# First layer of a two-layer trunk: from the third input slab on, pairs of slabs as seven block products of scaled float16 pairs

## The chip, the core and the metric

One core of a Trainium2 chip runs the kernel. The metric is the device time of one execution in microseconds (us). The kernel before takes 1219.48 us (median of 3 runs, 1219.08 to 1220.45). TensorE is written PE (its weight loads PEld), VectorE DVE, ScalarE ACT, GpSimd POOL, and the engine that issues the DMAs SP.

## What is computed

Two layers over 1024 tokens of 1024 channels, in float32. The change touches the first layer alone:

```python
h = x @ w_in                      # 1024 x 1024 times 1024 x 3072
u_main, q_mem, g_main, g_mem = h[..., :1024], h[..., 1024:1536], h[..., 1536:2560], h[..., 2560:]
y_main = causal_multiscale_pool(u_main)        # 4 groups of 256 channels, windows 2, 4, 8, 16,
                                               # then a 256 x 256 map per group and a scale per channel
y_mem = memory_attention(q_mem, mem, w_mem_kv) # 4 heads into 256 memory tokens
y = concat([y_main * silu(g_main), y_mem * silu(g_mem)])
x = layer_norm(ALPHA * x + y @ w_out)
```

The second layer has the same projection, a forgetting attention of 16 heads in place of the pooling, and its own memory attention.

## The kernel before

Everything is kept transposed: channels lie on the 128 partitions and tokens along the free axis. `w_in` is cut into 24 slabs of 128 output channels for each layer: slabs 0 to 7 give `u_main` (two for each pooling group), 8 to 11 the memory queries, 12 to 19 the main gates, 20 to 23 the memory gates.

To keep float32 precision, each operand stands as a high part in a reduced float32 (`hi`, matmul type f32) and two bfloat16 tiles, the rest (`lo`) and a rounded copy (`top`). `hi_lo` (L160 on) makes them: two casts on ACT (L162, L164) and a subtraction on DVE (L163). A product is three: hi by hi, top by lo, lo by top (`three`). `slab` (L191 on) so issues 48 matmuls of 512 columns (L214): 2 halves of the tokens, 8 blocks of the inner dimension, 3 products. The weights of a slab come as two pieces of 128x512 through `split_w`: a DMA into the ring `raw` (4 tiles), then `hi_lo` into the ring `w` (6 tiles, two for a piece).

The first layer goes in this order. `load_x` brings the eight blocks of x, 512 KB each, and splits them, the `top` cast on POOL. `pool_group(0)` runs slabs 0 and 1 while x arrives, then the sums over the window (L554, a chain of additions of a tile with itself shifted, all on DVE), two gate slabs (12, 13) and the 256 x 256 map (L191, 24 matmuls). `mem_kv` projects keys and values of the memory tokens (eight projections of 24 matmuls of 256 columns, L248); `mem_attention` runs the four query slabs between them, and then the attention of eight token tiles, in which four gate slabs (20 to 23) fill PE between the steps of the softmax (`Fill.pump`). `pool_group(1)` to `(3)` follow, each with two slabs, two gates and its map; `OutProj.split` prepares pieces of `w_out` meanwhile (12 of 24 by the end of group 3, the rest in `OutProj.rest`), in tiles that `w_slots` takes from rings that are free by then (`wtags`, one of its entries, "PG", takes a tile of the rings P and G). `OutProj.rest` multiplies by `w_out` (L441), `norm` (L485 on, its tile `z` from the ring G, 4 tiles) normalizes and the result is transposed on PE (L294) as the input of the second layer.

Inside `mem_attention` the order on PE is the order of the program (`manual_schedule`); elsewhere, and on the other engines always, a scheduler orders the instructions before the run, by readiness in its own model and place in the program. On the chip every engine takes its instructions in that fixed order, and SP issues the DMAs in a fixed order too.

Of the kernel before, what the change touches and what calls it, by code (L numbers as in the profile page):

```python
# [9 lines left out]
F32 = mybir.dt.float32  # L10
# [8 lines left out]
P = 128  # L19
S = 1024  # L20
# [46 lines left out]
def run(units):  # L67
    for _ in units:
        pass
# [3 lines left out]
def trunk_kernel(ctx, tc, x, xT, memT, win, wk, wv0, wv, wmk, wmv, wout, poolw, pscale, lng, lnb, bforget, out):  # L73
# [24 lines left out]
    def sb(shape, tag, bufs, dt=F32, where=None):  # L98
        return (where or pool).tile(shape, dt, tag=tag, name=nm(tag), bufs=bufs)
# [4 lines left out]
    def G(shape=(P, S), dt=F32):  # L104
        return sb(list(shape), "G", 4, dt)

    def T(shape=(P, S), dt=F32R):
        return sb(list(shape), "T", 6, dt)

    def MK(shape, dt=F32R):  # L110
        return sb(list(shape), "MK", 4, dt)

    def raw(shape):
        return sb(list(shape), "raw", 4)

    def wt(shape, dt=F32R):
        return sb(list(shape), "w", 6, dt)
# [32 lines left out]
    def parts_of(make, shape):  # L150
        return Split(make(shape), make([shape[0], 2] + list(shape[1:]), BF16))
# [7 lines left out]
    def hi_lo(to, src, pinned=False, top=None):  # L159

        pin = tc.keep_in_program_order if pinned else lambda ins: ins
        pin(nc.scalar.copy(to.hi, src))  # L162
        pin(nc.vector.tensor_tensor(to.lo, src, to.hi.bitcast(F32), ALU.subtract))  # L163
        (top or nc.scalar.copy)(to.top, src)  # L164
# [6 lines left out]
    def split_w(src_dram, shape):  # L171
        r = raw(shape)
        nc.sync.dma_start(r, src_dram)
        to = parts_of(wt, shape)
        (gp_hi_lo if low[0] else hi_lo)(to, r)
        return to
# [43 lines left out]
                    yield NH  # L220

    SLAB = 48 * NH

    def gate(acc, dst):

# [80 lines left out]
    def gate_units(w_dram, dst, X):  # L306
        return slab(w_dram, X, lambda cols, acc: gate(acc, dst[:, cols]))

    def mem_attention(l, X, kv, qtile, ytile, yd):

        (mk, v, undo), keys, vals = kv
        qs = []
        if l:
            for h in range(MH):
                keys(h)
        for h in range(MH):
            while turns:
                spread()
            q = parts_of(qtile, [P, S])
            run(slab(win[l, 8 + h], X, lambda cols, acc: hi_lo(q[:, cols], acc)))  # L320
            qs.append(q)
            if not l:
                keys(h)
            vals(h)
        ys, gs = [ytile() for _ in range(MH)], [G() for _ in range(MH)]
        pt, fill = {}, Fill()
        for h in range(MH):
            fill.add(gate_units(win[l, 20 + h], gs[h], X), SLAB)

        def probs(i):  # L330

# [179 lines left out]

    X = parts_of(stream, [P, KT, S])

    def load_x(kt, parts=1):
        r = T(dt=F32)
        for i in range(parts):
            cols = slice(i * S // parts, (i + 1) * S // parts)
            nc.sync.dma_start(r[:, cols], xT[kt, :, cols])
            hi_lo(X[:, kt, cols], r[:, cols], top=gp_copy)

    first = [[split_w(win[0, 0, 0], [P, 4, P])], []]
    load_x(0, 2)
    first[1].append(split_w(win[0, 1, 0], [P, 4, P]))
    for kt in range(1, 4):
        load_x(kt)
    for f in range(2):
        first[f].append(split_w(win[0, f, 1], [P, 4, P]))
    for kt in range(4, KT):
        load_x(kt)
    nc.sync.dma_start(psc, pscale)  # L530
    nc.vector.tensor_scalar(pschalf, psc, 0.5, None, ALU.mult)
# [5 lines left out]
    with tc.tile_pool(name="in0", bufs=1) as in0:  # L537

        def bt(shape=(P, S), dt=F32R):
            return sb(list(shape), "B", 8, dt, in0)  # L540

        def pool_group(g):
            w = WINDOWS[g]
            pms = []
            for f in (2 * g, 2 * g + 1):
                u = sb([P, S], "P", 4)
                run(slab(
                    first[f] if g == 0 else win[0, f], X, lambda cols, acc: nc.scalar.copy(u[:, cols], acc),
                    ("L", 3) if f == 1 else ("pj", 2),
                ))  # L550
                cur, sh = u, 1
                while sh < w:
                    nxt = G()
                    nc.vector.tensor_tensor(nxt[:, sh:], cur[:, sh:], cur[:, : S - sh], ALU.add)  # L554
# [5 lines left out]
                nc.vector.tensor_tensor(pm[:, : w - 1], pm[:, : w - 1], u[:, : w - 1], ALU.subtract)  # L560
                pms.append(parts_of(T, [P, S]))
                hi_lo(pms[-1], pm)
            r = raw([P, 2, 2 * P])
            nc.sync.dma_start(r, poolw[g])
            w2 = parts_of(MK, [P, 2, 2 * P])
            hi_lo(w2, r)
            ys = []
            for f in (2 * g, 2 * g + 1):
                y = sb([P, S], "Y", 4, F32, in0)
                run(gate_units(win[0, 12 + f], y, X))  # L570
                ys.append(y)
# [22 lines left out]
        out_proj.rest(x, X1, x1)  # L594


    X = X1
    with tc.tile_pool(name="in1", bufs=1) as in1:
# [8 lines left out]
            return sb(shape, "V", 4, dt, in1)  # L607

        kv = mem_kv(1)
        mem_attention(1, X, kv, xy, lambda: vt([P, S], F32), y1d[2])  # L610
        cumd = dram.tile([HEADS, S], F32, name="cumd")
        fg = G((P, 8, ST * HEADS))
        flog = fg[:, 0, :]
# [406 lines left out]
```

## Time and profile before

| | |
|---|---|
| time, median of 3 runs | 1219.48 us |
| the profiled execution: its own time | 1218.15 us |
| its span, first to last instruction | 1216.4 us |
| PE busy | 1193.7 us (98%) |
| DVE, ACT, POOL busy | 793.3, 697.4, 221.0 us |
| POOL busy from 20 us to the end of the first layer | 0 |

The trace lists each instruction with its engine, line, start and length. A row of the view by lines gives a group's count, its busy time and the mean length of one in ns. Matmuls overlap in their pipeline, so the pace of a stream is read from the starts of successive rows and not from the length of one matmul. The stages of the first layer stand in the trace at: 0 to 32.5 us slabs 0 and 1 with the loading of x; to 59.1 the rest of group 0; to 123.3 queries and memory projections; to 187.5 the memory attention; to 330.5 groups 1 to 3; to 463 the output projection with the norm.

### The profile page before, as it was taken

What the parts mean: (1) busy time and instruction counts of PE and PEld (TensorE: products, weight loads), DVE (VectorE), ACT (ScalarE), POOL (GpSimd) and SP (SyncE); (2) the same over time, 40 slices, a digit from 0 to 9 for tenths busy, and PEclk for the clock granted to TensorE, in tenths of its full rate; (3) what the DMA queues carried; (4) which work ended last, traced back from release to release, by engine and by line L of the source; (5) the groups of instructions that cost most, each with busy time, mean ns of one, the idle gap of its engine ahead of it and who ended that gap; (6) DMA issues with size and microseconds to landing.
All of it is one profiled execution on the core that took longest, in us unless ns stands there. A gap on an engine that the chain in (4) does not pass through costs nothing. (4 is left out here: it accounts for less than half of the span.)

```text
span 1216.4 us, 20026 instructions
## 1 busy us (share of the span) xinstructions
PE 1193.7 (98%) x7018; PEld 758.7 (62%) x7018; DVE 793.3 (65%) x1853; ACT 697.4 (57%) x1474; POOL 221.0 (18%) x349
## 2 busy tenths in 40 slices
PE   9999999999999998999999999999999999999996
PEld 4566666555555666667686666666666666665553
DVE  7534676475644457357736888878877888874754
ACT  6556774374542345567533777767776777685220
POOL 4000000000000000000002454544444434640000
PEclk9999999999999999999999999999999999999999
DMA  6232553232452333234517879988887989895340
GB/s 229 84 112 95 122 131 139 95 121 88 164 182 104 111 129 116 70 96 109 159 52 181 162 161 194 181 187 172 182 195 159 193 188 229 222 241 195 132 156 36
DMA packets 267414, 178.68 MB, mean 147 GB/s; under 512 B 212272, under 2 KB 225712, under 8 KB 267312
## 3 DMA queue, kind: packets, MB, share of 16 engines
q1 hardware_dynamic: 267312, 177.40, 56.2%
q8 instruction: 55, 0.90, 0.3%
q14 instruction: 47, 0.39, 0.1%
HBM read 94.97 MB, written 22.61 MB: 97 GB/s over the span
## 5 line engine op out<-in xcount | busy, mean ns | idle before, releaser
L214 PE MATMUL pj<-A,w 128*128 128x512 bf16 (+1 forms) x2928 | 684.7, 390 | 3.1 <-DVE B L724 1.6
L214 PEld LDWEIGHTS <-w 128*128 128x128 bf16 x1984 | 182.3, 98 | 223.8 <-issue 23.3
L214 PEld LDWEIGHTS pj<-A,w 128*128 128x128 f32 x976 | 181.1, 189 | 45.8 <-ACT A L162 2.8
L789 ACT ACTIVATE T<-MK,s 128x512 f32<-128x512 f32 x192 | 111.3, 580 | 41.5 <-DVE s L781 23.6
L811 DVE SCALAR_TENSOR_TENSOR P<-T,s,P 128x512 f16<-128x512 f32 x192 | 111.6, 613 | 34.7 <-ACT P L810 33.4
L163 DVE TENSOR_TENSOR w<-raw,w 128x512 bf16<-128x512 f32 x106 | 75.6, 714 | 83.6 <-PE pj L214 51.5
L810 ACT ACTIVATE P<-T,s 128x512 f16<-128x512 f32 x192 | 103.0, 576 | 46.0 <-ACT T L789 20.1
L441 PEld LDWEIGHTS <-T 128*128 128x128 bf16 x736 | 70.7, 98 | 82.9 <-issue 3.7
L191 PE MATMUL L<-B,B 128*128 128x512 f32 (+3 forms) x384 | 105.8, 381 | 2.2 <-DVE s L781 2.1
L686 POOL MEMSET G<- 128x128 f32 x1 | 0.2, 208 | 581.5 <-ACT MK L164 581.5
L191 PEld LDWEIGHTS L<-B,B 128*128 128x128 f32 x384 | 70.8, 189 | 22.9 <-DVE s L781 4.8
L162 ACT CAST w<-raw 128x512 fp32r<-128x512 f32 x106 | 65.9, 621 | 26.6 <-PE pj L214 14.6
L157 POOL TENSOR_SCALAR w<-raw 128x512 fp32r<-128x512 f32 x108 | 67.3, 629 | 65.0 <-PE pj L214 59.7
L781 DVE CUSTOM_DVE_ANT_0 MK<-L,R 128x512 f32<-128x512 f32 (+3 forms) x128 | 72.5, 566 | 8.7 <-PE L L191 6.9
L164 ACT CAST w<-raw 128x512 bf16<-128x512 f32 x106 | 65.7, 620 | 18.9 <-PE pj L214 18.2
L773 POOL TENSOR_SCALAR_AFFINE_SELECT R<-R 128x128 f32<-128x128 f32 x128 | 41.3, 328 | 174.4 <-DVE s L781 129.4
L168 POOL TENSOR_TENSOR w<-raw,w 128x512 bf16<-128x512 f32 x54 | 69.6, 1288 | 18.7 <-PE pj L214 16.2
L163 DVE TENSOR_TENSOR T<-T,T 128x1024 bf16<-128x1024 f32 x23 | 28.0, 1218 | 52.2 <-ACT T L162 36.9
L833 PE MATMUL O<-T,V 128*64 128x128 f16 (+1 forms) x1152 | 57.6, 220 | 2.7 <-DMA T<-P 2.5
L833 PEld LDWEIGHTS <-V 128*64 128x64 f16 (+1 forms) x1152 | 50.2, 104 | 15.2 <-issue 5.7
L162 ACT CAST T<-T 128x1024 fp32r<-128x1024 f32 x23 | 24.1, 1046 | 60.3 <-DMA T<-y1d 33.9
L441 PE MATMUL pj<-B,T 128*128 128x512 bf16 (+1 forms) x192 | 52.6, 383 | 0.0
(230 smaller groups left out, 1699.3 us busy)
## 6 DMA issues: line engine op xcount, KB each, us to landing
raw<-in_win_dram SPq DMA_DIRECT2D x96, 256.0 KB, 2.8
raw<-in_wout_dram SPq DMA_DIRECT2D x40, 256.0 KB, 2.8
B<-B SPq DMA_DIRECT2D x32, 256.0 KB, 4.2
R<-cumd SPq DMA_DIRECT2D x16, 512.0 KB, 5.0
y0d<-Y SPq DMA_DIRECT2D x12, 512.0 KB, 3.1
T<-y0d SPq DMA_DIRECT2D x12, 512.0 KB, 3.8
T<-y1d SPq DMA_DIRECT2D x11, 512.0 KB, 4.9
raw<-in_wmk_dram SPq DMA_DIRECT2D x16, 256.0 KB, 2.6
```

The costliest lines, as they stand in the source:

```text
L157: nc.gpsimd.tensor_scalar(to, src, 1.0, 1.0, ALU.mult, ALU.mult)
L162: pin(nc.scalar.copy(to.hi, src))
L163: pin(nc.vector.tensor_tensor(to.lo, src, to.hi.bitcast(F32), ALU.subtract))
L168: nc.gpsimd.tensor_tensor(to.lo, src, to.hi.bitcast(F32), ALU.subtract)
L191: nc.tensor.matmul(acc, a, b, start=i == 0, stop=i == len(terms) - 1)
L214: nc.tensor.matmul(accs[n], a[:, k, :], b[:, pc * 4 + k, n * NH : (n + 1) * NH], start=seen[n] == 1, stop=seen[n] == 3 * KT,)
L441: nc.tensor.matmul(accs[a][nh], y, w, start=kt == 8 and i == 0, stop=kt == 7 and i == 2,)
L781: nc.vector.tensor_tensor_reduce(p[:, lo:up], lg, R[:, lo:up], 1.0, top, ALU.add, ALU.min, m[:, n : n + 1])
L789: nc.scalar.activation(e, p[:, lo:up], AF.Exp, bias=top, scale=-1.0, accum_out=sums[:, n, hd % 2, i : i + 1],)
L810: nc.scalar.activation(pair[:, lo:up], e, AF.Copy, scale=r)
L811: nc.vector.scalar_tensor_tensor(pair[:, L + lo : L + up], e, r, pair[:, lo:up], ALU.mult, ALU.subtract)
L833: nc.tensor.matmul(acc[rows, (i % 4) * P : (i % 4) * P + P], v[:, b, 2 * j : 2 * j + (1 if e else 2), :].rearrange("p e d -> p (e d)"), pt ...
```

## The change

Slabs 0 and 1 of the first layer stay as they were. The other 22 slabs go in eleven pairs. A pair is a product of 256 output channels by 1024 inner channels by 1024 tokens; it is cut into 2 x 2 blocks and done by seven block products in the place of eight (Strassen's scheme in Winograd's form). A block product is 128 outputs, 512 inner channels and 512 tokens.

The operands are now pairs of float16: a tensor is scaled by a power of two from its largest sum of absolute values, cast on ACT, and the rest taken by one DVE instruction (`halves_of`). Three products (high by high, high by rest, rest by high) make a block product 12 matmuls of 512 columns, and a pair 84.

- The blocks of x: seven combinations, made once (`combine`): 16 additions of 128x512 on POOL, and `halves_of` 28 times on 128x512. They lie in the tiles that held X. The blocks of x stay in the ring B till then.
- The blocks of the weights: for each pair four DMAs into `raw` (now 6 tiles), four ACT passes for the sums of absolute values, `bound` (a column of 128 maxima to DRAM and back to all partitions), four subtractions of 128x512 on POOL, and seven `halves_of` into `w` (now 8 tiles, one for a block).
- The results: running sums stay in PSUM where they can, and the others are read by ACT (2 for each pair) or by a DVE instruction that scales and adds (5 for each pair). The gate's tanh and product then work on SBUF tiles.
- The order: the eight memory projections now follow slabs 0 and 1 at once, each with a step of `combine`; the query pairs, gate pair and map of group 0 come behind them. In this stretch and in groups 1 to 3 PE's order is that of the program.
- Pooling: of the two window sums of a group the second runs on POOL (`pooled`).
- The output weights: 8 pieces by the end of group 3 in the place of 12; the ring W is gone, "PG" stands twice and the ring `w` twice in `wtags`.

```diff
+    def bound(sums):
+        m, e = tiny(1), tiny(1)
+        d = dram.tile([P, 1], F32, name=nm("bound"))
+        nc.vector.tensor_reduce(m, sums, AX.X, ALU.max)
+        nc.sync.dma_start(d, m)
+        every = sb([P, P], "every", 2, F32, more[0])
+        nc.sync.dma_start(every, d.rearrange("p o -> (p o)").partition_broadcast(P))
+        nc.vector.tensor_reduce(m, every, AX.X, ALU.max)
+        nc.vector.tensor_scalar(m, m, 2.0 ** -100, None, ALU.max)
+        nc.vector.tensor_scalar(e.bitcast(I32), m.bitcast(I32), 0x7F800000, None, ALU.bitwise_and)
+        return e
+
+    def scale_of(e, name):
+        sc = sb([P, 1], name, 3, F32, more[0])
+        nc.vector.reciprocal(sc, e)
+        nc.vector.tensor_scalar(sc, sc, 2.0 ** 12, None, ALU.mult)
+        return sc
+
+    def halves_of(to, src, sc):
+        nc.scalar.activation(to[:, 0], src, AF.Copy, scale=sc)
+        nc.vector.scalar_tensor_tensor(to[:, 1], src, sc, to[:, 0], ALU.mult, ALU.subtract)
+
+    def slab_pair(one, two, XC, dest, done):
+        combos, xun, ts = XC
+        b11, b12, b22, b21 = bs = [raw([P, 4, P]) for _ in range(4)]
+        sums = tiny(4)
+        for b, src in zip(bs, (one[0], two[0], two[1], one[1])):
+            nc.sync.dma_start(b, src)
+        for j, b in enumerate(bs):
...
+            nc.scalar.activation(junk, b, AF.Abs, accum_out=sums[:, j : j + 1])
+        e = bound(sums)
+        sc = scale_of(e, "wsc")
+        un = sb([P, 1], "wun", 3, F32, more[0])
+        nc.vector.tensor_tensor(un, e, xun, ALU.mult)
+        t1, t2, t3, t4 = ts
+        for to, a, b in ((t1, b12, b11), (t2, b22, t1), (t3, b22, b12), (t4, b21, t2)):
+            nc.gpsimd.tensor_tensor(to, a, b, ALU.subtract)
...
+        def plus(to, acc, other):
+            nc.vector.scalar_tensor_tensor(to, acc, un, other, ALU.mult, ALU.add)
...
+        steps = ((b11, "a", 1), (t2, "b", 1), (b21, "a", 0), (t1, "b", 0), (t3, "c", 1), (b22, "b", 0), (t4, "c", 0))
+        for k, (src, name, opens) in enumerate(steps):
+            w, xc = wt([P, 2, 4, P], F16), combos[k]
+            halves_of(w, src, sc)
+            if opens:
+                bank[name] = ps([P, NH], "pj", 2)
+            for i, (e0, e1) in enumerate(((0, 0), (0, 1), (1, 0))):
+                for kt in range(4):
+                    nc.tensor.matmul(
+                        bank[name], w[:, e0, kt, :], xc[:, e1, kt, :],
...
+                    if i == 2 and kt == 3:
+                        evac(k)
+                    yield NH
...
-                cur, sh = u, 1
+            for u, eng in zip(us, (nc.vector, nc.gpsimd)):
+                cur, sh = u, 1
                 while sh < w:
                     nxt = G()
-                    nc.vector.tensor_tensor(nxt[:, sh:], cur[:, sh:], cur[:, : S - sh], ALU.add)
-                    nc.vector.tensor_copy(nxt[:, :sh], cur[:, :sh])
+                    eng.tensor_tensor(nxt[:, sh:], cur[:, sh:], cur[:, : S - sh], ALU.add)
+                    eng.tensor_copy(nxt[:, :sh], cur[:, :sh])
...
+        for kt in range(KT):
+            junk = sb([P, S], "e", 3, BF16, in0)
+            nc.scalar.activation(junk, xs[kt], AF.Abs, accum_out=sums[:, kt : kt + 1])
+        e = bound(sums)
+        xsc = scale_of(e, "xsc")
...
+        quads = [sb([P, 4, 2, 4, NH], "A", 2, F16) for _ in range(2)]
...
+        changes = {0: ((b21, b21, b22, ALU.add), (b11, b21, b11, ALU.subtract)), 3: ((b21, b22, b11, ALU.subtract),), 2: ((b12, b12, b11, ALU.subtract),)}
+
+        def combine(k):
+            src = (b11, b11, b12, b21, b21, b12, b22)[k]
+            for kt in range(4):
+                halves_of(XC[0][k][:, :, kt, :], src[kt], xsc)
+            for to, a, b, op in changes.get(k, ()):
+                for kt in range(4):
+                    nc.gpsimd.tensor_tensor(to[kt], a[kt], b[kt], op)
+
+        with tc.manual_schedule(engines={PE}):
+            kv = mem_kv(0)
+            for h in range(2 * MH):
+                kv[1 + h // MH](h % MH)
+                if h:
+                    combine(h - 1)
+            pms = pooled(0, us)
+            qs = [parts_of(bt, [P, S]) for _ in range(MH)]
+            for h in (0, 2):
+                wide = [G() for _ in range(2)]
+                run(plain_pair(8 + h, wide, lambda j, cols, t: hi_lo(qs[h + j][:, cols], wide[j][:, cols])))
+            ys = [y_tile() for _ in range(2)]
+            run(gate_pair(12, ys))
+            pool_out(0, pms, ys)
+        mem_attention(qs, kv, lambda gs: [gate_pair(20 + h, gs[h : h + 2]) for h in (0, 2)], PAIR, y_tile, y0d[2])
 
-        wtags = [("B", 8)] * 4 + [("W", 4)] * 2 + [("MK", 4), ("w", 0)] + [("Y", 4)] * 2 + [("PG", 0), ("MK", 4)]
+        wtags = [("B", 8)] * 4 + [("MK", 4), ("w", 0), ("w", 0)] + [("Y", 4)] * 2 + [("PG", 0)] * 2 + [("MK", 4)]
         out_proj = OutProj(0, w_slots(wtags, in0), y0d)
-        pool_group(0)
-        kv = mem_kv(0)
-        mem_attention(0, X, kv, bt, lambda: sb([P, S], "Y", 4, F32, in0), y0d[2])
-        for g in range(1, 4):
-            pool_group(g)
-            out_proj.split((4, 12, 12)[g - 1])
+        with tc.manual_schedule(engines={PE}):
+            for g in range(1, 4):
+                us = [u_tile() for _ in range(2)]
+                run(plain_pair(2 * g, us))
+                pms = pooled(g, us)
+                ys = [y_tile() for _ in range(2)]
+                run(gate_pair(12 + 2 * g, ys))
+                pool_out(g, pms, ys)
+                out_proj.split((4, 8, 8)[g - 1])
```

More of the change, by code (lines that the diff above doesn't have):

```diff
@@ L321, in mem_attention @@
             qs.append(q)
-            if not l:
-                keys(h)
             vals(h)
+        return qs
+    def mem_attention(qs, kv, gates, cols_of_gate, ytile, yd):
+        mk, v, undo = kv[0]
         ys, gs = [ytile() for _ in range(MH)], [G() for _ in range(MH)]
         pt, fill = {}, Fill()
-        for h in range(MH):
-            fill.add(gate_units(win[l, 20 + h], gs[h], X), SLAB)
+        for units in gates(gs):
+            fill.add(units, cols_of_gate)
         def probs(i):
@@ new lines, in gate_pair, with done, plain_pair @@
+        def gate_pair(f, ys):
+            def done(j, cols, t):
+                y = ys[j][:, cols]
+                nc.scalar.activation(t, y, AF.Tanh, scale=0.5)
+                nc.vector.scalar_tensor_tensor(y, t, 1.0, y, ALU.add, ALU.mult)
+            return slab_pair(win[0, f], win[0, f + 1], XC, lambda j, cols: ys[j][:, cols], done)
+        def plain_pair(f, us, done=lambda j, cols, t: None):
+            return slab_pair(win[0, f], win[0, f + 1], XC, lambda j, cols: us[j][:, cols], done)
@@ new lines, in trunk_kernel @@
+        us = [u_tile() for _ in range(2)]
+        for f in range(2):
+            run(slab(
+                first[f], X, lambda cols, acc: nc.scalar.copy(us[f][:, cols], acc), ("L", 3) if f == 1 else ("pj", 2),
+            ))
+        sums = sb([P, KT], "xsums", 1, F32, in0)
+        for kt in range(KT):
[3 more added lines that the diff above has]
+        xsc = scale_of(e, "xsc")
```

125 lines of the change are left out of this document (85 added, 40 removed).

## The prediction

> **What bounds the kernel now.** I read the page's busy times first, then PE's timeline through the first layer, then the busy times by stage.
>
> ```profile
> span 1216.4 us, 20026 instructions
> PE 1193.7 (98%) x7018; PEld 758.7 (62%) x7018; DVE 793.3 (65%) x1853; ACT 697.4 (57%) x1474; POOL 221.0 (18%) x349
> ```
>
> ```profile
> 32.52 21.53 PE L214 MATMUL pj<-A,w 128*128 128x512 f32 x96
> 69.87 5.57 PE L248 MATMUL pj<-T,w 128*128 128x256 f32 x48
> 75.27 10.76 PE L214 MATMUL pj<-A,w 128*128 128x512 f32 x48
> ...
> 182.16 1.51 PE L191 MATMUL T<-T,MK 128*128 128x128 f16 x24
> 183.51 1.50 PE L191 MATMUL O<-T,MK 128*128 128x128 f16 x24
> 187.50 42.58 PE L214 MATMUL pj<-A,w 128*128 128x512 f32 x192
> 229.92 5.54 PE L191 MATMUL L<-T,MK 128*128 128x512 f32 x24
> 235.10 1.28 PE L214 MATMUL pj<-A,w 128*128 128x512 f32 x4
> ...
> 334.36 1.90 PE L441 MATMUL L<-B,T 128*128 128x512 bf16 x8
> 336.09 1.89 PE L441 MATMUL pj<-B,T 128*128 128x512 bf16 x8
> ```
>
> The columns are start, length, engine, line and count. Successive rows start where the last block's pace says they should: a group's 192 slab matmuls take 229.92 - 187.50 = 42.42 us, its map 5.18. PE waits for nobody here.
>
> ```profile
> 22.00:123.30 101.30, 100.47 (x550) 64.18 (x549) 48.26 (x91) 57.17 (x106) 0.00 (x0) 1.00 0.31 97
> 124.60:187.50 62.90, 62.90 (x471) 43.68 (x469) 45.54 (x112) 43.36 (x124) 0.00 (x0) 1.00 0.52 129
> 187.50:330.50 143.00, 143.00 (x652) 80.88 (x650) 85.83 (x131) 74.75 (x124) 0.00 (x0) 1.00 0.34 114
> ...
> 463.00:482.00 19.00, 15.05 (x113) 13.03 (x112) 15.21 (x33) 14.55 (x31) 0.00 (x0) 0.91 0.41 123
> ```
>
> Columns: stretch, its length, then the busy time of PE, PEld, DVE, ACT and POOL, the granted clock, DMA. PE fills the three stages that the change rewrites; DVE stands at 48, 72 and 60%, ACT at 56, 69 and 52%, POOL does nothing. What PE saves is saved outright, as long as DVE and ACT can carry what they are given.
>
> **What is saved on PE.** A pair of slabs now takes 42.42 / 2 = 21.2 us. Eight bfloat16 matmuls of 512 columns take 336.09 - 334.36 = 1.73 us, 0.216 each. For float16 the nearest row is the 24 matmuls of 128 columns in 183.51 - 182.16 = 1.35 us, 0.056 each, four of which make 0.225; I take 0.216 (the other end costs 0.8 us a pair). A pair then takes 84 x 0.216 = 18.15 us. Eleven pairs: 11 x 3.06 = **33.7 us** off PE, 9.2 in the first stage (three pairs), 6.1 in the memory attention, 18.4 in groups 1 to 3. PE alone would need 92, 57 and 125 us there.
>
> **What DVE gets.**
>
> ```profile
> L285 DVE SCALAR_TENSOR_TENSOR MK<-MK,s,MK 128x1024 f16<-128x1024 f32 x8 | 10.3, 1282 | 2.0 <-ACT MK L284 2.0
> L352 DVE SCALAR_TENSOR_TENSOR P<-P,s,P 128x256 f16<-128x256 f32 x32 | 13.4, 482 | 2.5 <-ACT P L351 2.5
> L163 DVE TENSOR_TENSOR w<-raw,w 128x512 bf16<-128x512 f32 x9 | 6.2, 690 | 2.5 <-PE pj L214 1.1 <-ACT w L162 1.0
> ...
> L163 DVE TENSOR_TENSOR w<-raw,w 128x512 bf16<-128x512 f32 x23 | 15.9, 691 | 21.5 <-PE pj L214 18.3 <-ACT w L162 3.2
> L554 DVE TENSOR_TENSOR G<-G 128x1022 f32<-128x1022 f32 x6 | 7.3, 1222 | 0.2
> L554 DVE TENSOR_TENSOR G<-P 128x1023 f32<-128x1023 f32 x6 | 7.3, 1218 | 0.0
> ...
> L554 DVE TENSOR_TENSOR G<-G 128x1020 f32<-128x1020 f32 x4 | 4.9, 1218 | 0.1
> ...
> L554 DVE TENSOR_TENSOR G<-G 128x1016 f32<-128x1016 f32 x2 | 2.4, 1214 | 0.0
> ...
> L802 DVE RECIPROCAL s<-s 128x1 f32<-128x1 f32 x128 | 20.8, 162 | 3.1
> ```
>
> The scaled subtraction of `halves_of` is the operation of L285 and L352: between 256 and 1024 columns it grows by 800 ns, so 512 take 0.75 us. `plus` is the same operation with PSUM as one source. A pair has 7 + 5 of them, 9.0 us, and seven short ones of the kind of L802, 1.1: 10.1 us. Back to back they overlap a little (L352: 32 x 0.482 = 15.4 us long, 13.4 busy), so I count 0.9 of that, **9.1 us a pair**, and for the 28 `halves_of` of x 28 x 0.75 x 0.9 = **18.9 us**. Gates keep their DVE instruction. What goes: the pieces of the weights (L163, 0.69 each: 12 in the first stage, the 9 and 23 of the rows in the others), half of the window sums (half of the rows' 21.9 us in groups 1 to 3, with nine short copies, 1.4 by L802's length; 1.4 in group 0) and four pieces of `w_out` (2.8). By stage:
>
> - first stage: 48.3 - 8.3 - 1.4 + 3 x 9.1 + 18.9 = 85 us
> - memory attention: 45.5 - 6.2 + 2 x 9.1 = 57.5 us, as long as PE's 57
> - groups 1 to 3: 85.8 - 15.9 - 11.0 - 1.4 - 2.8 + 6 x 9.1 = 109 us
>
> **What POOL gets, and what it does to DVE.**
>
> ```profile
> L168 POOL TENSOR_TENSOR w<-raw,w 128x512 bf16<-128x512 f32 x54 | 69.6, 1288 | 18.7 <-PE pj L214 16.2 <-POOL w L157 0.3
> ```
>
> An addition of 128x512 is 1.29 us on POOL (L168), one of 1024 columns at most two of them. First stage: 16 for x and 12 for three pairs, 36 us, with one window sum 38.7; memory attention 8, 10.3 us; groups 1 to 3: 24 and nine window sums, 54. Together **103 us**. By itself this hides everywhere. But see what happens when the two engines work at once, while x arrives:
>
> ```profile
> 7.84 1.05 POOL L157 TENSOR_SCALAR A<-T 128x1024 bf16<-128x1024 f32 x1 [1.32 <-DMA T<-in_xT_dram]
> ...
> 9.08 10.74 POOL L157 TENSOR_SCALAR A<-T 128x1024 bf16<-128x1024 f32 x6 [0.18 <-DMA T<-in_xT_dram]
> ...
> 13.98 1.52 DVE L163 TENSOR_TENSOR w<-raw,w 128x512 bf16<-128x512 f32 x1
> ...
> 17.39 1.52 DVE L163 TENSOR_TENSOR w<-raw,w 128x512 bf16<-128x512 f32 x1
> ...
> 22.02 1.21 DVE L163 TENSOR_TENSOR A<-T,A 128x1024 bf16<-128x1024 f32 x1
> ...
> 23.76 0.68 DVE L163 TENSOR_TENSOR w<-raw,w 128x512 bf16<-128x512 f32 x1
> ```
>
> A cast that takes POOL 1.05 us alone takes 10.74 / 6 = 1.79 beside DVE; a DVE subtraction that takes 0.68 alone takes 1.52. Each has waited for the other: they take turns. These subtractions read two tensors in SBUF, and so do `halves_of` (the source and the high part), the pooling, the memory pieces, L352 and the gates; `plus` reads one of its two from PSUM; I count it as free of this, and f rises if it isn't. The two-SBUF kind is about 160 of DVE's 252 us, an estimate from the lengths above: 105 `halves_of` 71, L352 13, 20 memory pieces 14, 24 gate products at 0.69 17, pooling, queries and output pieces 45. So some share f of POOL's 103 us adds to DVE's time. Bounds: 0, if POOL's instructions all fall into DVE's idle time and its PSUM work, and 1. If DVE were never idle, f would be near 160 / 252 = 0.64; it is idle at times; I take **0.5**.
>
> The Trainium skill, page "SBUF — State Buffer", section "SBUF: two separate sides", calls the port pair that the two engines share "an exclusive lock, not a bandwidth split", for a DVE instruction with two SBUF inputs against a GpSimd one that reads SBUF, held for the whole instruction. This trace agrees: 0.68 + 0.84 = 1.52.
>
> **The sum.** First stage: 85 + 0.5 x 38.7 = 104 us of DVE from 22 us on. The tiles of X can't be rewritten before the last matmul of slabs 0 and 1 at 32.5 us, which leaves DVE some 6 us idle. ACT is nearly as full.
>
> ```profile
> L162 ACT CAST w<-raw 128x512 fp32r<-128x512 f32 x106 | 65.9, 621 | 26.6 <-PE pj L214 14.6 <-DMA raw<-in_win_dram 5.7 <-DMA raw<-in_wmk_dram 2.3
> L789 ACT ACTIVATION_READ_ACCUMULATOR T<-MK,s 128x1 f32 x192 | 36.5, 190 | 0.2
> L162 ACT CAST T<-G 128x1024 fp32r<-128x1024 f32 x8 | 8.4, 1046 | 5.1 <-DVE G L560 5.1
> ```
>
> 57.2 in its row, less 24 casts (14.9), and 28 x 0.62 for x (17.4), 8 x (1.05 + 0.19) for its sums (9.9) and three times 4 x 0.81 + 7 x 0.62 + 2 x 0.6 (26.4): 96 us, and each high part precedes its rest on DVE. Two engines that wait on each other at 90% don't mesh; I add 8 us. The stage ends at 22 + 104 + 6 + 8 = 140 us, where it ended at 123.3: **+17** (26 lost against PE's 92). PE waits in the projections and the first query pair.
>
> Memory attention: 57.5 + 5 = 62.7 against 62.9: **0**. Groups 1 to 3: 109 + 27 = 136 against 143: **-7**. Output projection: four more pieces to prepare behind group 3, and "PG" twice leaves `norm` two z tiles of four where it had three, so that the fourth row block's x is fetched only once a z is transposed. The nearest rows are the wait that follows this stage, 19 us with PE busy for 15.05, and nothing at all; I take **+4**. Together +14 on the profiled execution's 1218.15, 1232. The median of the runs is 1.3 above that execution, so **1233 us**.
>
> That stage shows a clock of 0.91 where PE idled; the Trainium skill, page "TensorE: Matmul & The Clock Gate", Part 1, has the clock halve after an idle window of about 3.4 us. By it the waits of the first stage would cost somewhat more; nothing above counts it.
>
> **The rivals.**
>
> 1. *PE stays the bound.* POOL's additions have a pair's time to be done (`w` holds 8 tiles, a pair needs 7), so they may fall where DVE reads PSUM or idles. For it: 160 + 103 us of turn-taking just fit under PE's 274. Against it: DVE alone is level with PE in the memory attention. Price: f near 0.15, and in the first stage ACT's 96 us from 22 us on, 4 above PE's 92, with 6 for X: -33.7 + 10 + 4 = -20, **1199 us**. It decides from f = 0.36 down, since each tenth of f is 10 us.
> 2. *No meshing at all.* The order on DVE is fixed before the run; where a subtraction stands at its head while POOL holds the port, the PSUM reads behind it wait too, and PE waits for its bank. f near 1: +14 + 51 = **1284 us**; with f = 0.8, 1264.
> 3. *The scale of each pair comes late.* `bound` puts two DMAs in a row on SP's queue, and the DVE reduction behind them holds up DVE's queue.
>
> ```profile
> cumd<-G SPq DMA_DIRECT2D x8, 8.0 KB, 2.0
> bfb<-in_bforget_dram SPq DMA_DIRECT2D x1, 8.0 KB, 2.6
> ```
>
> Four sums 3.2, two DMAs 4.6, short work 1.1 and a first high part and rest 1.4: 10.3 us for each pair. I hold it hidden, since the rings hold a pair ahead of 18 us. With no cover: 11 x 10.3 = 113 less 33.7, about **1299 us**.
> 4. *float16 doesn't keep bfloat16's pace:* 11 x 0.8 us more on PE, little here, where PE is not the bound.
>
> **How the numbers follow.** The forecast has 0.48, the first rival 0.27, the second 0.17, the third 0.05, the fourth 0.03. A measurement tells about 0.2%, 2.4 us, from no change. The forecast's own range is f from 0.3 to 0.7, 1213 to 1253; most of it is slower (0.43), a little the same (0.03) or faster (0.02). With the first rival faster 0.30, same 0.04, slower 0.66. The range for 8 in 10 takes in most of the first rival and the lower half of the second: 1201 to 1265.
>
> **What would show it.** Right: DVE near 90% busy, its waits included, from 30 us to the end of group 3; `halves_of` beside POOL above 1.2 us where alone it takes 0.75; POOL's additions stretched past 1.29; PE gaps in the memory projections and the first query pair, released by ACT and DVE; the first matmul of L441 near 340 us. Wrong: seven block products in 18.2 us back to back in groups 1 to 3 (first rival), or PE waiting at each pair's first product for a DVE instruction that waits for a DMA (third).

## The result, and the profile after

The changed kernel takes **1399.97 us** (median of 4 runs, 1395.51 to 1403.29) against 1219.28 for the kernel before (4 runs): **1.148 times** as long, 95% interval 1.144 to 1.152. That is slower, as forecast, but by 181 us where 14 were predicted, and far outside the range. The profiled execution took 1397.46 us.

First the page of the changed kernel: span, busy times, and two of the rows of 40 slices (tenths).

```profile
span 1395.8 us, 20190 instructions
PE 1202.3 (86%) x6886; PEld 726.7 (52%) x6886; DVE 908.1 (65%) x2033; ACT 758.4 (54%) x1605; POOL 337.1 (24%) x429
...
PE   8635857557776689998999999999999999999997
...
PEclk9777988788998889999999999999999999999999
```

PE stands idle for 1395.8 - 1202.3 = 193.5 us, where it stood idle for 1216.4 - 1193.7 = 22.7: 171 us more. No other engine is full. And PE's busy time rose by 8.6 us where 33.7 were to be saved: the slices with holes in PE are also those with a clock of 0.7 to 0.9, most of them 0.7 and 0.8. The work itself keeps the pace that was predicted. The timeline of PE for one pair (start, length, engine, line, count):

```profile
139.14 5.34 PE L314 MATMUL pj<-A,wx 128*128 128x512 f16 x24
144.32 1.89 PE L314 MATMUL pj<-A,w 128*128 128x512 f16 x8
```

24 matmuls in 144.32 - 139.14 = 5.18 us, 0.216 each. So float16's pace is not why PE's busy time misses its saving by 42 us; the lower clock is what the page shows beside it. After a wait the same work is slower: at 427.91 us, behind a wait of 9.81, 24 such matmuls take 7.09 us, and the granted clock between 427.9 and 435.3 us is 0.71. The stages (busy time of PE, PEld, DVE, ACT and POOL, clock, DMA; the first row is the stretch from 22 us to the first matmul of the memory attention, then one window within it, then the attention, then groups 1 to 3):

```profile
22.00:191.90 169.90, 111.74 (x521) 59.37 (x519) 102.16 (x174) 89.81 (x169) 45.78 (x31) 0.81 0.31 58
50.00:100.00 50.00, 28.30 (x161) 20.83 (x159) 45.17 (x74) 39.08 (x73) 22.46 (x15) 0.74 0.26 79
191.90:299.40 107.50, 62.62 (x458) 38.94 (x456) 59.83 (x135) 52.41 (x146) 14.66 (x11) 0.79 0.39 69
299.40:501.80 202.40, 140.65 (x580) 60.78 (x578) 132.08 (x203) 90.35 (x161) 54.78 (x38) 0.85 0.35 80
```

The three stages grew by 69, 43 and 59 us (from 101.3, 64.2 and 143.0), what comes behind them by 8. In none is an engine near full over the whole stage: this is waiting, in a place with little slack. The view of the waits of 90 to 500 us says on what (engine, line, released by: us in total, times, longest; waits of POOL and PEld are left out):

```profile
...
DVE s L242 <- DMA every<-bound: 72.4, 10, 13.4
ACT wx L254 <- DVE wsc L250: 48.8, 4, 14.6
...
PE pj L314 <- ACT wx L254: 43.0, 2, 22.5
...
PE pj L314 <- ACT w L254: 36.2, 2, 22.7
...
PE pj L314 <- DVE e L279: 22.0, 7, 6.0
...
PE pj L314 <- DVE s L243: 9.8, 1, 9.8
```

Read it as a chain: PE waits for ACT's first high part (L254), ACT for the scale (L250), DVE for the load in `bound` (L242). PE also waits for DVE instructions that have nothing to do with the scale (L279, the reading of a bank). Not all of that is the exchange's: 16.5 of these 22.0 us lie in groups 1 to 3, where the kernel without the exchange (experiment 1) has 17.3 for the same instruction. But a DVE instruction that waits for the exchange holds up whatever stands behind it in DVE's fixed order: at 371.88 us L242 has waited 6.91 us for its load, and PE then goes on after a wait of 5.65 us for an instruction behind it (L680, which reads the bank of the map). The exchange itself, in the view of the tile `bound` (count, ns to issue, first and last; who waited; from issue to landing, store and load together):

```profile
L239 SPq DMA_DIRECT2D bound<-s x12: 319/329/562, 31.1 to 444.6; - x12
L241 SPq DMA_DIRECT2D every<-bound x12: 320/326/327, 38.6 to 452.4; - x12
...
  DVE s L242: 81.3, 11
...
DMA to landing us min/median/max: 3.3/6.0/9.4
```

The first store is issued at 31.1 us and its load at 38.6: 7.5 us in between; over the twelve the distance is 7.2 to 9.4, and from the store to the reduction 11.6 to 13.3. The prediction had 4.6 for both DMAs. What a single exchange does in groups 1 to 3 stands in the timeline:

```profile
320.67 0.33 SPq L239 DMA_DIRECT2D bound<-s  x1
321.10 1.06 SPq L508 DMA_DIRECT2D raw<-in_wout_dram  x2
...
322.39 5.34 PE L314 MATMUL pj<-A,w 128*128 128x512 f16 x24
...
328.60 0.33 SPq L241 DMA_DIRECT2D every<-bound  x1
331.52 0.62 ACT L171 CAST B<-raw 128x512 fp32r<-128x512 f32 x1 [8.25 <-DMA raw<-in_wout_dram]
...
332.18 0.69 DVE L172 TENSOR_TENSOR B<-raw,B 128x512 bf16<-128x512 f32 x1 [8.71 <-ACT B L171]
...
333.18 0.28 DVE L242 TENSOR_REDUCE s<-every 128x1 f32<-128x128 f32 x1 [0.31 <-DMA every<-bound]
...
334.19 0.74 DVE L279 SCALAR_TENSOR_TENSOR e<-pj,wun,e 128x512 f32<-128x512 f32 x1
...
334.98 2.29 PE L314 MATMUL pj<-A,w 128*128 128x512 f16 x5 [7.25 <-DVE s L244]
```

PE's block ends at 327.73. The read of its bank (L279) comes only at 334.19, and PE goes on when it is done, at 334.93 (the trace puts the wait down to L244, which ends at about the same moment). Two things stand before that read in DVE's order. The first is the subtraction for a piece of `w_out` (L172), for which DVE waits 8.71 us: the loads of `w_out`, issued at 321.10 behind the store, are late, and the ACT cast before the subtraction waits 8.25 us for one. The second is the reduction of the *next* pair's scale, for which DVE then waits only 0.31 us more. So here the store does its harm through the loads behind it; at 394.36 and 455.27 us ACT waits 6.36 and 11.23 us for such loads in the same way. The view of the DMAs of 320 to 334 us has their times from issue to landing:

```profile
raw<-in_wout_dram SPq DMA_DIRECT2D x3, 256.0 KB, 10.3
every<-bound SPq DMA_DIRECT2D x1, 64.0 KB, 4.5
bound<-s SPq DMA_DIRECT2D x1, 0.5 KB, 7.9
```

A store of half a kilobyte takes 7.9 us, and loads issued behind it 10.3, where the median over the run for such a load is 3.1.

### The profile page after: what moved, and what is told of

It is laid out like the page before. It is cut to its first block, busy times and chain, and to the rows that moved or that the text cites. A ratio compares the mean times of both kernels' runs of the same rounds, so it can differ in the third digit from the quotient of the medians.

```text
span 1395.8 us, 20190 instructions
## 1 busy us (share of the span) xinstructions
PE 1202.3 (86%) x6886; PEld 726.7 (52%) x6886; DVE 908.1 (65%) x2033; ACT 758.4 (54%) x1605; POOL 337.1 (24%) x429
## 5 line engine op out<-in xcount | busy, mean ns | idle before, releaser
L223 PE MATMUL pj<-A,w 128*128 128x512 bf16 (+1 forms) x1872 | 448.6, 391 | 5.3 <-ACT A L171 2.4
L314 PE MATMUL pj<-A,w 128*128 128x512 f16 x696 | 172.8, 410 | 87.8 <-ACT w L254 36.2
L223 PEld LDWEIGHTS <-w 128*128 128x128 bf16 x1264 | 114.0, 98 | 140.6 <-issue 19.4
L314 PEld LDWEIGHTS <-w 128*128 128x128 f16 x696 | 72.3, 104 | 184.6 <-issue 78.6
L978 DVE SCALAR_TENSOR_TENSOR P<-T,s,P 128x512 f16<-128x512 f32 x192 | 111.5, 613 | 34.8 <-ACT P L977 33.5
L223 PEld LDWEIGHTS pj<-A,w 128*128 128x128 f32 x624 | 115.2, 190 | 31.0 <-ACT A L171 4.6
L314 PE MATMUL pj<-A,wx 128*128 128x512 f16 x228 | 54.3, 394 | 46.4 <-ACT wx L254 43.0
L347 PE MATMUL pj<-T,w 128*128 128x256 bf16 (+1 forms) x336 | 51.5, 307 | 23.5 <-ACT w L173 6.9
L172 DVE TENSOR_TENSOR T<-T,T 128x1024 bf16<-128x1024 f32 x23 | 28.1, 1223 | 58.4 <-ACT T L171 36.4
L172 DVE TENSOR_TENSOR w<-raw,w 128x512 bf16<-128x512 f32 x55 | 42.0, 764 | 32.1 <-PE pj L223 14.8
L314 PEld LDWEIGHTS <-wx 128*128 128x128 f16 x228 | 22.8, 101 | 75.6 <-ACT wx L254 43.8
```

The lines of the kernel that those rows point to most:

```text
L223: nc.tensor.matmul(accs[n], a[:, k, :], b[:, pc * 4 + k, n * NH : (n + 1) * NH], start=seen[n] == 1, stop=seen[n] == 3 * KT,)
L314: nc.tensor.matmul(bank[name], w[:, e0, kt, :], xc[:, e1, kt, :], start=bool(opens) and i == kt == 0, stop=k in (2, 5, 6) and i == 2 and k ...
L978: nc.vector.scalar_tensor_tensor(pair[:, L + lo : L + up], e, r, pair[:, lo:up], ALU.mult, ALU.subtract)
```

## The experiments

The theory: the exchange of the scale sets the time, through its own length and through the queues that it holds. The rivals: the turns that POOL and DVE take (the prediction's own term), and plain work on ACT or DVE. Ratios are to the kernel before on the same chip, with the 95% interval; differences are given in us of 1219.

**1. No exchange.** `bound` keeps its first reduction and gives a constant.

```diff
-        nc.sync.dma_start(d, m)
...
-        nc.vector.tensor_scalar(e.bitcast(I32), m.bitcast(I32), 0x7F800000, None, ALU.bitwise_and)
+        nc.vector.tensor_scalar(e, m, 0.0, known, ALU.mult, ALU.add)
```

> The exchange of the maximum over the partitions through DRAM is left out: the sums and the first reduction stay, and the scale is a constant, the one that the exchange gives for this data (512 for x, 8 for each pair). In the changed kernel each of the 12 exchanges takes 11.6 to 13.3 us from the store's issue to the reduction of what came back, and DVE stands at that reduction. Theory A (the exchange, by the queues that it holds, is what PE waits for): 120 to 160 us fall away, 1240 to 1280. Theory B (DVE and GpSimd in turn, as the prediction has it): at most 40 us, 1360 or more. Theory C (the preparation of a pair starts too late whatever it holds): about half, 1310 to 1340.

1292.4 us, 1.061 [1.059, 1.064]: 106 us of the 181 are the exchange. The time lies between the ranges of theories A and C.

**2. The exchange made, its result unused.** Constant scale as in 1, but both DMAs and the reduction stay.

```diff
         nc.vector.tensor_reduce(m, sums, AX.X, ALU.max)
+        nc.vector.tensor_scalar(e, m, 0.0, known, ALU.mult, ALU.add)
         nc.sync.dma_start(d, m)
```

> The exchange stays in its queues, two DMAs on SP and the reduction on DVE, but nobody uses what it brings: the scale is the constant of the run without it. Theory A1 (the exchange hurts because the instruction that waits for it holds up DVE's and SP's queues): most of the loss stays, 1340 to 1390. Theory A2 (it hurts because the scale comes late): the time of the run without the exchange, within 15 us.

1355.1 us, 1.112 [1.110, 1.115]. So of the 106 us, 62 are there though nobody needs the scale (what waits behind the exchange on DVE, on SP and among the DMAs), and 44 come with the lateness of the scale itself.

**3. The additions of W back on DVE**, with the exchange (`e3`) and without (`e4`).

```diff
-            nc.gpsimd.tensor_tensor(to, a, b, ALU.subtract)
+            nc.vector.tensor_tensor(to, a, b, ALU.subtract)
```

> The 44 subtractions of W move from GpSimd to DVE, where one takes about 0.69 us; the exchange stays. Theory A: DVE waits idle for the exchange and has room, so 1385 to 1415, as the changed kernel within 1%. Theory B: the turns with GpSimd fall away in the pairs, 80 us or more, 1320 or less.

> Both edits: no exchange and the subtractions of W on DVE. Against the run without the exchange alone this prices the turns that DVE and GpSimd take in the pairs: by the prediction's f of 0.5, 57 us of GpSimd work cost 28 us and 30 us of DVE work come back, so the two are within 10 us of each other; if the port doesn't matter, this run is 10 to 25 us slower.

1393.3 us, 1.144 [1.141, 1.146], whose interval overlaps that of the change; and 1286.2 us, 1.056 [1.054, 1.058], 6 us below experiment 1. Having W's additions on GpSimd costs some 6 us, with the exchange and without.

**4. No sums at all.** No exchange, no ACT passes for the sums, a constant set by a memset.

```diff
-            nc.scalar.activation(junk, b, AF.Abs, accum_out=sums[:, j : j + 1])
...
-        nc.vector.tensor_reduce(m, sums, AX.X, ALU.max)
...
+        nc.vector.memset(e, known)
```

> Without the exchange, and the passes that sum absolute values are left out too (four on ScalarE for a pair, eight for x, and their reductions): the scales are constants that wait for nothing. Theory C1 (what is left, 73 us over the kernel before, is a pair's preparation that starts late, since the sums stand late in ScalarE's order): 40 us or more below 1292, 1250 or less. Theory C2 (it is the work on DVE and GpSimd in the first stage): ScalarE loses 45 us of work, DVE next to nothing, 10 to 20 us, 1270 to 1282.

1264.5 us, 1.037 [1.035, 1.039]: 29 us below experiment 1 and between the ranges of C1 and C2. The passes are 4 x 0.81 us for each pair on ACT, but the next experiment keeps them and wins nearly as much.

**5. The sums in a ring of their own**, on top of 1.

```diff
-        sums = tiny(4)
+        sums = sb([P, 4], "wsums", 3, F32, more[0])
```

> Without the exchange, and a pair's tile of four sums gets a ring of its own. In the kernel it comes from the ring of four tiles from which each softmax step takes all four (maximum, scaled maximum, sum, reciprocal), so that a gate pair that is emitted behind a softmax step can't start its sums before that step is over: in the run without the exchange they start at 162.8 us, as the last exponential ends, though the weights have long landed. Theory C1 with this cause: the waits of 9.6 and 8.0 us at the start of the two gate pairs of the memory attention go, 12 to 25 us, 1267 to 1280, and the stage (158.4 to 245.4 us there) shrinks to 62 to 75 us. Theory C2: nothing, 1288 to 1297.

1267.9 us, 1.040 [1.039, 1.042], 25.6 us below experiment 1 from this one line. `tiny(4)` shares a ring of four tiles with the softmax of the memory attention. The timeline of experiment 1 shows it:

```profile
162.72 0.21 ACT L440 ACTIVATION_READ_ACCUMULATOR P<-L,s 128x1 f32 x1
162.82 0.64 ACT L260 ACTIVATE A<-raw 128x512 bf16<-128x512 f32 x1
...
167.35 1.26 POOL L267 TENSOR_TENSOR A<-raw,raw 128x512 f32<-128x512 f32 x1 [37.00 <-ACT A L260]
```

The sums of the next gate pair (L260) begin as soon as the softmax's last exponential has been accumulated (L440), and POOL has been waiting for them for 37 us. With its own ring the memory attention takes 68.1 us instead of 84.9.

**6. Other work away from GpSimd**, each on top of 1: the second window sum (`e7`), the additions of x (`e8`), and all of it, with W's additions and the ring of 5 (`e9`).

```diff
-            for u, eng in zip(us, (nc.vector, nc.gpsimd)):
+            for u, eng in zip(us, (nc.vector, nc.vector)):
...
-                    nc.gpsimd.tensor_tensor(to[kt], a[kt], b[kt], op)
+                    nc.vector.tensor_tensor(to[kt], a[kt], b[kt], op)
```

> Without the exchange, and the second window sum of a group goes back from GpSimd to DVE: ten additions of 1024 columns, 1.22 us each on DVE, over 2 us on GpSimd. If the turns of the two engines set the time of groups 1 to 3, 5 to 15 us are won, 1277 to 1287; if DVE's own work does, 5 to 12 us are lost, 1297 to 1305.

> Without the exchange, and the 16 additions for x on DVE: 11 us of DVE work for 20 us of GpSimd work in the first stage. If the chain through GpSimd and the turns set the start of the first query pair (94.6 us in the run without the exchange), it comes 5 to 12 us earlier, 1280 to 1287; if DVE's own work does, it comes up to 10 us later, 1295 to 1303.

> Without the exchange, own ring for the sums, and all three kinds of work that the change gave to GpSimd on DVE (additions of W, additions for x, second window sums). Added up from the single runs: 1268 less 6, 6 and 15, so 1241. If the turns of the two engines overlap with other waits and the three shares aren't additive: 1247 to 1260. Below 1219 only if the first stage's wait goes too, which nothing here touches but the additions for x.

1277.2 us, 1.048 [1.046, 1.050]; 1286.6, 1.056 [1.054, 1.058]; and with all of it 1239.4, 1.017 [1.015, 1.019], 28.4 us below experiment 5; the single shares, 6 (`e4`), 16 and 7, add up to it. DVE gets more to do and the kernel is faster. The turns are one reason. Another is that the work itself gets shorter (a subtraction of W takes 1.26 us on POOL and 0.68 on DVE) and that POOL drops out of the chain; no run separates the two, though no wait of PE in the change or in experiment 5 is put down to POOL. `halves_of` in the views of its line, first the changed kernel, then `e9` with GpSimd idle in the whole stretch (ns, min/median/max):

```profile
L255 DVE SCALAR_TENSOR_TENSOR w<-A,wsc,w x35: 739/747/2384, 114.4 to 467.5; 128x512 f16<-128x512 f32 x35
L255 DVE SCALAR_TENSOR_TENSOR A<-B,xsc,A x28: 733/742/1833, 49.4 to 92.3; 128x512 f16<-128x512 f32 x28
```

```profile
L249 DVE SCALAR_TENSOR_TENSOR w<-A,wsc,w x35: 739/746/753, 88.0 to 317.4; 128x512 f16<-128x512 f32 x35
L249 DVE SCALAR_TENSOR_TENSOR A<-B,xsc,A x28: 736/744/753, 39.9 to 79.9; 128x512 f16<-128x512 f32 x28
```

Alone 0.75 us, never more; beside GpSimd up to 2.4.

**7. With the exchange: its own ring (`e12`), and GpSimd idle too (`e10`).**

> The changed kernel with one edit, the own ring for the sums, exchange and GpSimd work kept. If the ring costs what it costs without the exchange: 1370 to 1380. If the sums' late start in the memory attention exposes the whole exchange there (waits of 22.7 and 20.7 us): 1345 to 1365.

> As the run with no GpSimd work and the own ring, but with the real exchange through DRAM. If the exchange costs what it cost in the changed kernel (108 us): 1345 to 1355. If half of that cost came from the late start of the gate pairs of the memory attention, whose sums now start earlier: 1300 to 1330.

1359.6 us, 1.116 [1.114, 1.119], and 1335.6 us, 1.097 [1.094, 1.099]. The ring costs 39 us here, against 26 without the exchange, and `e12` lies in the second of its ranges: the late start of the sums exposes part of the exchange too. GpSimd's work costs 24 us, about what it cost without (28). Taking both away doesn't hide the exchange: `e10`, between its two ranges, and `e9` differ in the exchange alone and lie 98 us apart.

**8. What of the exchange is slow.** Its store writes one float of each of 128 partitions. As 128 rows of 512 bytes (`e11`, on top of 2, one run), and as 4 rows of 128 bytes, after a transposition on DVE, with the scale taken from the data (`e13`, the change with this alone). The two edits:

```diff
-        nc.sync.dma_start(d, m)
+        nc.vector.tensor_copy(rows[:, 0:1], m)
+        nc.sync.dma_start(d, rows)
```

```diff
-        nc.sync.dma_start(d, m)
+        blocks = [sb([P, 32], "blocks", 2, F32, more[0]) for _ in range(2)]
+        nc.vector.tensor_copy(blocks[0], m.broadcast_to([P, 32]))
+        nc.vector.transpose(blocks[1], blocks[0])
+        nc.sync.dma_start(d, blocks[1][0:P:32, :])
```

> The exchange without a user, but its store writes 128 rows of 512 bytes (the maximum and zeros) in the place of 128 rows of 4 bytes, and the load reads one row of 512 bytes for all partitions as before. If rows of 4 bytes are what makes the store land late, the load issues about 2 us after the store, where it was 7.2 to 9.4 us in the changed kernel; if any store followed by a load of the same place takes that long, 7 us or more again.

> The changed kernel with one edit: the 128 maxima are spread over 32 columns and turned in blocks of 32x32 on VectorE (two short instructions more), so that the store writes 4 rows of 128 bytes in the place of 128 rows of 4 bytes; the load of the 512 bytes for all partitions and all that follows stays. If the rows of 4 bytes are the cost: the load issues 2 to 3.5 us after the store in the place of 7.2 to 9.4, the exchange takes 6 to 8 us, and 60 to 90 us fall away: 1310 to 1340. If the wait for any exchange in these queues is the cost, whatever its length: 1375 or more.

`e11` took 1291.7 us in its one run, as long as with no exchange at all (1292.4): the 62 us of experiment 2 are gone, though it moves 128 times the bytes. `e13`: 1318.4 us, 1.081 [1.079, 1.082], 82 us below the change. One exchange of `e13` in the timeline:

```profile
176.68 0.53 SPq L242 DMA_DIRECT2D bound<-blocks  x1
178.93 0.33 SPq L244 DMA_DIRECT2D every<-bound  x1
...
181.76 0.29 DVE L245 TENSOR_REDUCE s<-every 128x1 f32<-128x128 f32 x1 [5.28 <-DMA every<-bound]
```

2.25 us from store to load and 5.08 in all, where the same exchange took 8.89 and 13.27 in the change; over the twelve it is 4.7 to 8.4 in all. DVE waits 22.9 us for them where it waited 81.3.

**9. The best with everything computed**: short store, own ring, GpSimd idle.

> The short store, the own ring for the sums and no GpSimd work: the real computation with its real scale. With an exchange of 6 to 8 us: between the run without any exchange (1239) and the one with the long store (1336), 1255 to 1280. At or below 1219 it would beat the kernel before; the first stage, 26 us longer than before even without an exchange, speaks against it.

1259.9 us, 1.033 [1.031, 1.034]: 140 us below the change, and still 40 above the kernel before. None of the kernels run beats that one.

**10. What is left in the first stage.** `e9` without sums (`e15`), and `e9` without the rests of x (`e16`).

```diff
-                halves_of(XC[0][k][:, :, kt, :], src[kt], xsc)
+                nc.scalar.activation(XC[0][k][:, 0, kt, :], src[kt], AF.Copy, scale=xsc)
+                nc.vector.memset(XC[0][k][:, 1, kt, :], 0.0)
```

> No exchange, no GpSimd work, and no passes for the sums of absolute values (45 us of ScalarE work less, a quarter of it before the first pair); the scales are constants. If ScalarE sets the first stage (85% busy there in the run with the sums): 10 to 20 us less, 1220 to 1229, with a first stage of 108 to 117 us in the place of 127. If VectorE does: 1233 to 1240.

> No exchange, no GpSimd work, and the rests of the 28 pieces of x are zeros by a memset in the place of the scaled subtraction (the product of the high part of the weights with the rest of x is so left out). Some 14 us of VectorE work less before the first pair. If VectorE sets the first stage (90% busy there): 8 to 14 us less, 1225 to 1231; if ScalarE does: 1234 to 1240.

1233.4 us, 1.011 [1.009, 1.013], and 1236.9 us, 1.014 [1.012, 1.016]. The windows of `e9` by stage and in the middle of the first, and then that middle window in `e15` and in `e16`:

```profile
22.00:149.20 127.20, 103.17 (x515) 56.57 (x513) 106.96 (x212) 98.10 (x190) 0.00 (x0) 0.89 0.28 82
149.20:214.10 64.90, 61.65 (x469) 38.67 (x468) 60.49 (x147) 53.17 (x146) 0.00 (x0) 1.00 0.51 128
214.10:346.30 132.20, 126.21 (x568) 57.22 (x565) 121.35 (x206) 77.34 (x135) 0.00 (x0) 0.97 0.32 100
35.00:87.00 52.00, 30.76 (x192) 23.46 (x191) 48.62 (x104) 44.52 (x85) 0.00 (x0) 0.78 0.32 95
```

```profile
35.00:87.00 52.00, 33.38 (x208) 23.94 (x207) 50.65 (x110) 41.86 (x76) 0.00 (x0) 0.80 0.34 94
```

```profile
35.00:87.00 52.00, 32.31 (x198) 24.27 (x196) 39.62 (x107) 46.55 (x90) 0.00 (x0) 0.81 0.40 114
```

In `e9` groups 1 to 3 take 132.2 us, 10.8 less than before, and the attention about as long as before: what is left is in the first stage, 127.2 against 101.3, and some 9 us behind group 3. `e16` takes DVE from 48.6 to 39.6 us busy there and wins less than 1 us on the stage (126.5); `e15` takes ACT from 44.5 to 41.9 and wins 6.6 (120.6). PE's longest waits between 30 and 90 us of `e9`:

```profile
PE pj L341 <- ACT w L171: 10.6, 7, 3.8
PE pj L308 <- ACT w L248: 8.6, 1, 8.6
```

Both are casts on ACT. By the ranges set ahead, each run speaks against the engine that it relieves: `e16` lies where ACT was to set the stage, and `e15` at the edge of where DVE was, with a stage of 120.6 us where 108 to 117 was forecast for ACT. So neither engine's load alone sets this stage. The rows point to ACT's order; that is not shown, since no run changes that order alone.

## Why the prediction was wrong

One path of removals accounts for the whole difference, each step a difference of two measured ratios times 1219:

| | ratio | step, us |
|---|---|---|
| the change | 1.148 | |
| store in 4 rows, not 128 of 4 bytes (`e13`) | 1.081 | 82 |
| own ring for the sums, GpSimd idle (`e14`) | 1.033 | 58 |
| no exchange at all (`e9`) | 1.017 | 19 |
| no sums (`e15`) | 1.011 | 7 |
| what is left | | 14 |

**The step that failed is the third rival's**, "I hold it hidden, since the rings hold a pair ahead of 18 us", with its price, 4.6 us for two DMAs and a chance of 0.05.

- *The price.* It was taken from rows of 8 KB transfers (2.0 and 2.6 us). The store is smaller by a factor of 16, but it consists of 128 rows of 4 bytes, and store and load together took 11.6 to 13.3 us. A transfer of 16 times the bytes was no bound. That the rival's 113 us without cover lie near the 106 of experiment 1 is luck: it counts the chain of a pair, and 62 of the 106 are there without any pair waiting for its scale. The Trainium skill, page "DMA: Bandwidth & Descriptors", section "Specifications", gives 512 B as the smallest transfer for full rate and says that below it the DMA engine does read-modify-write; it was there to be weighed. The runs agree in direction: 128 rows of 4 B took 7.9 us to land and 128 rows of 512 B 2.0. Few rows below 512 B were cheap all the same, as the 4 rows of 128 B show, behind which the load was issued after about 2.25 us. No run shows what happens inside the DMA engine.
- *The cover.* A ring that holds a pair ahead hides the lateness of a scale. It doesn't hide that the waiting instruction stands in front of others in a fixed order. Experiment 2 measured this part: 62 us with a scale that nobody waits for. The prediction's own sentence on this rival ("the DVE reduction behind them holds up DVE's queue") had the mechanism, and then counted only the pair's own chain. It also didn't ask what is behind the store among the DMAs: loads that landed after 10.3 us and held up ACT, DVE and PE in turn.
- *The rest of the cover.* The rings named were those of the operands. The tile of the sums, 4 floats wide, lies in a ring shared with the softmax, and so the gate pairs of the memory attention could not be prepared ahead: 26 us of the whole time alone (`e1` to `e6`), 39 with the exchange. "Memory attention: 0" failed by this.

**What held.** PE's saving: 0.216 us a matmul; in `e15` PE's busy time is 1168.7 us (its page), 25 less than before; the rest of the 33.7 stands beside a clock of 0.92 in its first stage. The turns of DVE and POOL: the mechanism is as told, with 103 us of POOL's work forecast and 337.1 - 221.0 = 116 measured. The two kernels that differ in where this work is done (`e6`, `e9`) lie 28.4 us apart, though `e9`'s DVE does the additions too. The prediction's f of 0.5 is 51 us of lengthened DVE work; 28.4 is a net figure, so f as such was not measured. The 0.84 in its "0.68 + 0.84 = 1.52" is what is left of 1.52, and no row of its own; the rows of experiment 6 are the better evidence. The Trainium skill, page "SBUF — State Buffer", section "SBUF: two separate sides", the lock cited there, agrees: 753 ns at most without GpSimd, 2384 beside it. The output projection's +4: from group 3's end to the end of the span it is 889.1 us in `e14` (1258.5 - 369.4), 891.9 in `e6` (1266.0 - 374.1), 894.0 in the change (1395.8 - 501.8) and 895.1 in `e9` (1241.4 - 346.3), against 885.9 before: +3 to +9.

**What was mis-sized besides.** Without the exchange and with the ring apart, the sum is still short. `e6`, which keeps POOL's work, is the kernel that the forecast describes, and it takes 1267.9 us where 1233 was forecast. Its first stage, memory attention and groups 1 to 3:

```profile
22.00:157.90 135.90, 104.31 (x516) 55.64 (x516) 111.54 (x180) 99.55 (x192) 55.66 (x37) 0.90 0.25 78
157.90:226.00 68.10, 63.30 (x468) 40.02 (x469) 60.74 (x137) 53.81 (x147) 13.08 (x9) 0.97 0.44 116
226.00:374.10 148.10, 128.66 (x564) 57.30 (x565) 126.43 (x174) 79.09 (x139) 49.68 (x34) 0.95 0.29 96
```

Against before they are 35, 4 and 5 us longer, where +17, 0 and -7 were forecast. Groups 1 to 3 show a gain, 10.8 us, only in `e9`, without POOL's work. In the first stage 18 us are missing. DVE is busy there for 111.5 us, where 104 were forecast, and idle for 24, where 6 + 8 were: some 8 of the 18 are DVE's own time, and some 10 are idle time, for which "I add 8 us" had no row. And the clock, which the prediction named and didn't count: 42 us of PE's busy time, in stages at 0.79 to 0.85, beside 171 us of waits.

The sign was right for a reason that was only a small part of the loss: of 181 us 24 to 28 come with the work that POOL shares with DVE, and some 101 are the exchange (82 and 19 in the table).

## What to carry to other kernels

Price a small DMA by the number and the size of its rows and not by its bytes, and from a measured transfer of its own kind; if there is none, the range is open at the top. For every added wait list what stands behind it on its engine, on the queue that issues it and among the DMAs: a result that is needed late doesn't help where the wait stands early in a fixed order. And when a stage is to run ahead, look at each of its tiles, the tiniest too, for a ring shared with the work it is to overtake.

## What the runs showed of the hardware

- A store of 128 rows of 4 bytes to DRAM took 7.9 us from issue to landing in the exchange shown (0.5 KB); the median of the change's between 100 and 400 us is 8.0. One of 128 rows of 512 bytes took 2.0 in `e11`, as the view of its DMAs between 100 and 400 us has it:

```profile
bound<-rows SPq DMA_DIRECT2D x10, 64.0 KB, 2.0
every<-bound SPq DMA_DIRECT2D x10, 64.0 KB, 3.0
```

- Loads issued behind the 4-byte store on the same queue landed after 10.3 us where 2.6 to 3.1 are usual. It goes with the 4-byte rows: between 100 and 400 us the median of the loads `raw<-in_win_dram` is 4.3 us in experiment 2 and 2.7 in `e11`, which differ in the store and what prepares it. That the DMA engines work on the store's rows meanwhile is the likely reason; no run here separates it from others.
- Between 50 and 100 us of the change PE was busy for 28.3 of 50 us, and the granted clock was 0.74; in the attention of `e9`, where it was busy for 61.65 of 64.9, it was 1.00. Behind a wait of 9.81 us 24 matmuls took 7.09 us at a clock of 0.71, where 24 took 5.18 at 1.00 (139.1 to 150 us). So here waits cost twice where they are many, once as waits and once as slower matmuls.
